# The turned residual in the place of the rounded sums, and the last round's weight sums by adding transfers

## The chip, the cores and the metric

The kernel runs on one core of a Trainium2 chip. The core has a matrix engine (PE, with weight loads shown as PEld), a vector engine (DVE), a scalar engine (ACT), GpSimd (POOL) and SyncE (SP). In this kernel SP and POOL do little but issue transfers (DMA). All engines work in the order in which their instructions stand, and wait for each other by semaphores. The metric is the device time of one execution in microseconds (us), the median of several.

## The reference

A trunk of two residual layers over 512 tokens of width 1024, in float32. Layer 0 mixes tokens by banded attention, layer 1 by a gated linear recurrence (RG-LRU). Behind each mixer stands the same MLP, and the change lies in the MLPs alone:

```python
for layer in range(2):
    h = h + mixer(rmsnorm(h, norm_mix[layer]))
    z = relu(rmsnorm(h, norm_mlp[layer]) @ w1[layer])     # 512x1024 @ 1024x4096
    h = h + (z * z) @ w2[layer]                           # 512x4096 @ 4096x1024
return rmsnorm(h, norm_final)
```

## The kernel before, in words

Each float32 product is made of three matmuls of rounded operands: every operand is split into a high part (a cast to float32r on ACT, tiles `wh`, `hnH`, `rH`, `h`, `hs`) and the rest (a subtraction on DVE, `wl`, `hnL`, `rL`, `l`, `ls`). Function `mm3`, lines 280 to 282, issues the three. So each weight block that is used costs ACT a cast (L178) and DVE a subtraction (L183), and both must be there before PE can use it.

In an MLP, `mlp(ly, norm)`, the residual is held with features in partitions (`hT`, two buffers `hx0` and `hx1`). The 4096 hidden features are 8 groups of 512. Group 0 is made plainly by four calls `up(0, j)`. The other seven (`group(p, g)`) and the whole down product use a seven-product scheme for two by two blocks: blocks of weights are called `11`, `12`, `21`, `22`, and beside them sums of blocks are multiplied. In the up products the right operand's sums are `rF[1]` to `rF[4]`, made in place of the residual (`right`) and split into `rH` and `rL` (`right_split`); they are used by the pieces `r1` to `r4` of every group. The weights' sums there are `s1` to `s4`; a tile `kept` holds `s1` and `22`, tiles `u` hold `11` and `12`.

The down product runs in four rounds p = 0 to 3, `round_(p)`. Each uses blocks `b11`, `b12`, `b22`, `b21` of `w2` (two halves of 128x1024 each, 512 KB per half) and four sums `t1` = 12 + 11, `t2` = 22 + t1, `t3` = t2 - 11, `t4` = 21 + t2. `load_down` loads a block on SP's queue; `first_sum` makes `t1` by a transfer on POOL's queue that adds one tile to another; `fetch` makes `t2` and `t3` by DVE (L173, L176) and `t4` by an adding transfer (L174). Rounds 0 to 2 alternate with the pieces of two up groups; round 3 has nothing beside it. A step of a round multiplies into PSUM banks `x`, `y` or `z`, which DVE adds to the result `d` (`read`, L747).

`fetch` is called three blocks ahead of use, and five buffers each hold the split weights `wh` and `wl`. `plan` is the list of blocks in order. Within this, a tile framework sets each engine's order by its own costs, and a tile that takes the place of another waits until all that read the other are done.

At the beginning of an MLP the residual is also turned to have tokens in partitions, as the start of the result `d` (function `turn`, called behind `up(0, 0)`): 16 DVE transposes of 128x256 (L733) into two tiles `turned`, then 32 transfers of 64 KB, 16 on SP's queue and 16 on POOL's (L740). The two tiles lie in the places of `b12` and `b22`, so those blocks can be loaded only once the 32 transfers have read them. `rH` has a place of its own of the same 16 KB per partition.

Of the kernel before, what the change touches and what calls it, by code (L numbers as in the profile page):

```python
# [10 lines left out]
F32 = mybir.dt.float32  # L11
F32R = mybir.dt.float32r
# [3 lines left out]
P = 128  # L16
# [24 lines left out]
def trunk(ctx: ExitStack, tc: tile.TileContext, xT, cols, gfin, win, wqkv, wo, rwin, rga, rgx, rwo, w1, w2, out):  # L41
# [61 lines left out]
    def two(t):  # L103
        return t.rearrange("p (k c) -> p k c", k=2)
# [4 lines left out]
    def rows(src):  # L109
        return src.rearrange("(k p) c -> p k c", p=P)  # L110

    def load_down(key, name):
        if key not in down:
            return
        both = state["raw"].tile([P, 2, 1024], F32, name=f"b{name}_{key[0]}{key[1]}", tag=f"b{name}")
        for h in range(2):
            raws[name, h] = both[:, h]
            nc.sync.dma_start(two(raws[name, h]), rows(down[key][name][h * U : (h + 1) * U]))

    def first_sum(key):  # L120
        if key in down:
            for h in range(2):
                G.dma_start(raws["12", h], raws["11", h], accum_op=ALU.add)

    def load_up(key, name):
        if key not in upper:
            return
        if name in ("s1", "22"):
            raw = state["kept"][:, int(name == "22")]
        else:  # L130
            n = state["base"] + int(name == "12")
            raw = wraw.tile([P, 1024], F32, name=f"u{name}_{key[0]}{key[1]}", tag=f"wr{n % 3}")
        raws["u" + name] = raw
        nc.sync.dma_start(four(raw), rows(upper[key]["21" if name == "s1" else name]))
        if name == "s1":
            G.dma_start(four(raw), rows(upper[key]["22"]), accum_op=ALU.add)

    def fetch():
        i = state["next"]
        state["next"] += 1  # L140
        kind, nk, key = plan[i]
        H = wsp.tile([P, 1024], F32R, name=f"wh{i}", tag="wh")
        L = wsp.tile([P, 1024], F32R, name=f"wl{i}", tag="wl")
        n, half = 1024, nk
        if kind[:5] == "plain":
            n = nk * sum(src.shape[1] for src in key)
            raw = wraw.tile([P, 1024], F32, name=f"wr{i}", tag=f"wr{state['plain'] % 3}")
            state["plain"] += 1
            rv = raw[:, :n].rearrange("p (k c) -> p k c", k=nk)
            c0 = 0  # L150
            for n_, src in enumerate(key):
                w = src.shape[1]
                queue = nc.scalar if i == 0 and n_ else nc.sync
                queue.dma_start(rv[:, :, c0 : c0 + w], rows(src))
                c0 += w
        elif kind[0] == "u":
            nk = 4
            following = (key[0], key[1] + 1)
            if kind == "us2":
                raws["us2"] = wraw.tile([P, 1024], F32, name=f"us2_{key[0]}{key[1]}", tag=f"wr{(state['base'] + 2) % 3}")  # L160
                tc.keep_in_program_order(V.tensor_add(raws["us2"], raws["u11"], raws["us1"]))
                raws["us3"] = raws["u11"]
                G.dma_start(four(raws["us3"]), rows(upper[key]["21"]), accum_op=ALU.add)
            if kind == "us4":
                raws["us4"] = raws["u12"]
                V.tensor_add(raws["us4"], raws["us4"], raws["us2"])
            raw = raws[kind]
        else:
            nk = 2
            following = (key[0], key[1] + 1)  # L170
            raw = raws[{"t1": "12", "t2": "22", "t3": "11", "t4": "21"}.get(kind, kind), half]
            if kind == "t2":
                V.tensor_add(raw, raw, raws["12", half])  # L173
                G.dma_start(raws["21", half], raw, accum_op=ALU.add)  # L174
            if kind == "t3":
                V.tensor_sub(raw, raws["22", half], raw)  # L176
        if i:
            high = S.copy(H[:, :n], raw[:, :n])  # L178
            if kind in ("us1", "us3", "t1", "t4"):
                tc.keep_in_program_order(high)  # L180
        else:
            start_.append(V.tensor_copy(H[:, :n], raw[:, :n]))
        low = V.tensor_sub(L[:, :n], raw[:, :n], f(H[:, :n]))  # L183
        if not i:
            start_.append(low)
        if kind == "plain_":
            state["base"] = state["plain"] % 3
            load_up((nk_layer[i], 0), "11")
            load_up((nk_layer[i], 0), "12")
        elif kind == "us2" and key[1]:  # L190
            load_up(following, "s1")
        elif kind == "us3":
            load_up(following, "11")
        elif kind == "us4":
            load_up(following, "12")
        elif kind == "u22" and key[1]:
            load_up(following, "22")
        elif kind == "t2" and half:
            load_down(following, "12")
        elif kind == "t3" and half:  # L200
            load_down(following, "11")
        elif kind == "t4" and half:
            first_sum(following)
            load_down(following, "22")
            load_down(following, "21")
        state["ready"].append((nk, H[:, :n].rearrange("p (k c) -> p k c", k=nk), L[:, :n].rearrange("p (k c) -> p k c", k=nk)))

# [465 lines left out]
    def mlp(ly, norm):  # L673
        with ExitStack() as mctx:
# [3 lines left out]
            xs = [(hnH[k], hnL[k]) for k in range(KT)]  # L678
            res = dp.tile([P, 4, 2, T], F32, name=f"d{ly}", tag="d")
            dt = {(t, c): res[:, t, c] for t in range(4) for c in range(2)}  # L680
            rH = zp.tile([P, 4, 4, U], F32R, name=f"rH{ly}", tag="rH")
            rL13 = zp.tile([P, 2, 4, U], F32R, name=f"rL13{ly}", tag="rL")
            low_, high = hB[0], hB[1]
            rF = {1: low_[:, :, LO], 3: low_[:, :, HI], 4: high[:, :, LO], 2: high[:, :, HI]}
# [11 lines left out]
                    V.scalar_tensor_tensor(rF[n], rF[1 if n == 2 else 2], -1.0, rF[n], ALU.mult, ALU.subtract)  # L696

            def right_split(n):
                if n == 2:
                    rL24 = per.tile([P, 2, 4, U], F32R, name=f"rL24{ly}", tag="hx0")  # L700
                    rL.update({2: rL24[:, 0], 4: rL24[:, 1]})
                H = rH[:, n - 1]
                S.copy(H, rF[n])
                V.tensor_sub(rL[n], rF[n], f(H))

            def operand(n):
                if n[0] == "r":
                    H, L = rH[:, int(n[1]) - 1], rL[int(n[1])]
                    return [(H[:, k], L[:, k]) for k in range(4)]
                ks, c = (range(4) if n[0] == "1" else range(4, KT)), (LO if n[1] == "1" else HI)  # L710
                return [(hnH[k][:, c], hnL[k][:, c]) for k in ks]
# [15 lines left out]


            def turn():
                blocks = [sr.tile([P, 2, 4, KT, 32], F32, name=f"turned{ly}{h}", tag=f"b{n}2") for h, n in enumerate((1, 2))]  # L730
                for k in range(KT):
                    for h in range(2):
                        V.transpose(  # L733
                            blocks[h].rearrange("p t j k a -> p (t j) k a")[:, :, k],
                            hT[k][:, h * U : (h + 1) * U].rearrange("p (n b) -> p n b", b=32),
                        )
                for h in range(2):
                    for i in range(4):
                        for j in range(4):
                            (G if j % 2 else nc.sync).dma_start(  # L740
                                res[32 * j : 32 * j + 32, 2 * h : 2 * h + 2, i // 2, (i % 2) * U : (i % 2 + 1) * U],
                                blocks[h][32 * i : 32 * i + 32, :, j].rearrange("p t k a -> p t (k a)"),
                            )
# [39 lines left out]
            def first():  # L783
                state["kept"] = sr.tile([P, 2, 1024], F32, name=f"kept0{ly}", tag="b21")
                load_up((ly, 0), "s1")
                load_up((ly, 0), "22")
                for j in range(4):
                    up(0, j)
                state["kept"] = per.tile([P, 2, 1024], F32, name=f"kept{ly}", tag="hx1")
                load_up((ly, 1), "s1")  # L790
                load_down((ly, 0), "11")
                load_down((ly, 0), "12")
                first_sum((ly, 0))
                here = group(0, 1)
                next(here)
                opening(0)
                next(here)
                load_down((ly, 0), "22")
                for n in range(4):
                    next(here)  # L800
                load_down((ly, 0), "21")
                load_up((ly, 1), "22")
                next(here)
                sums(0, False)
                sums(0, True)
                lengths()
# [468 lines left out]
```

## Time and profile before

| | |
|---|---|
| time, median of 3 runs | 1044.04 us (1043.4 to 1046.31) |
| the profiled execution: time / span | 1043.58 / 1041.8 us |
| mean granted PE clock | 0.994 |
| busy: PE, DVE, ACT, POOL | 1024.3, 875.2, 665.4, 91.2 us |
| transfers | 147.33 MB, mean 141 GB/s |

Times in the views count from the span's start; the profiled execution's own time lies 1.78 us above its span. A row of the timeline gives start, duration, engine, line and what the instruction writes and reads; the bracket is the idle time of the engine just before and what ended it. "SPq" and "POOLq" rows are transfers being issued, not being carried out.

### The profile page before, as it was taken

The page shows a single profiled execution, that of the slowest core. Times are in us where ns is not written, and L with a number is a line of the kernel's source. Part 1 is how long each engine was busy: PE and PEld are TensorE (multiplying, and loading weights), DVE is VectorE, ACT ScalarE, POOL GpSimd, SP SyncE. Part 2 cuts the span into 40 slices and gives each one's busy share as a digit, 9 for nine tenths or more (in the row PEclk, how much of TensorE's full clock was granted, in tenths as well). Part 3 has the DMA queues.
Part 4 walks back from the last instruction along what each step waited for, and adds up shares of the span by engine and source line. Part 5 has one row for each costly group of instructions (what it writes and reads, how often), then busy time and mean ns, then how long its engine had stood idle before and what let it go on. Part 6 is the DMA issues. An engine that isn't in the chain of part 4 may idle for free.

```text
span 1041.8 us, 15285 instructions
## 1 busy us (share of the span) xinstructions
PE 1024.3 (98%) x5762; PEld 894.6 (86%) x5762; DVE 875.2 (84%) x1230; ACT 665.4 (64%) x1020; POOL 91.2 (9%) x120
## 2 busy tenths in 40 slices
PE   9999999999989999999999999999999999999996
PEld 8888888888979999999987788888999999999985
DVE  7998778869579899799789999888589798798697
ACT  7666556647477557557556686656586566566465
POOL 1000000003101111111000000003101111111000
PEclk9999999999999999999999999999999999999998
DMA  8444354245928828818603422284928738737412
GB/s 269 118 126 137 82 158 126 62 140 135 267 66 215 230 42 208 236 41 206 199 12 100 139 61 75 60 243 122 281 52 232 203 69 215 203 62 201 122 46 96
DMA packets 122729, 147.33 MB, mean 141 GB/s; under 512 B 6304, under 2 KB 94368, under 8 KB 122656
## 3 DMA queue, kind: packets, MB, share of 16 engines
q1 hardware_dynamic: 101664, 112.09, 34.5%
q0 software_dynamic: 20416, 33.56, 18.6%
q8 instruction: 45, 0.74, 0.3%
q10 hardware_dynamic: 576, 0.72, 0.2%
q14 instruction: 28, 0.23, 0.1%
HBM read 119.07 MB, written 2.10 MB: 116 GB/s over the span
## 4 chain that ended last, share of the span: by engine, by line
PE 86%; DVE 5%; DMA 3%; ACT 3%; issue 2%; ACTq 0%; DVEq 0%; SPq 0%
PE m L282 8%; PE m L281 8%; PE m L280 8%; PE x L280 5%; PE x L281 5%; PE x L282 5%; PE y L281 4%; PE y L282 4%; PE y L280 4%; DMA u<-in_w 2%; DVE wl L183 2%; PE x L506 2%; PE wo L280 1%; PE wo L281 1%; PE ro L282 1%
## 5 line engine op out<-in xcount | busy, mean ns | idle before, releaser
L183 DVE TENSOR_TENSOR wl<-b,wh 128x1024 fp32r<-128x1024 f32 x112 | 135.8, 1220 | 37.1 <-ACT wh L178 37.0
L178 ACT CAST wh<-b 128x1024 fp32r<-128x1024 f32 x112 | 116.3, 1050 | 66.1 <-PE m L281 18.9
L282 PE MATMUL m<-rH,wl 128*128 128x256 f32 x448 | 126.2, 282 | 0.0
L281 PE MATMUL m<-rL,wh 128*128 128x256 f32 x448 | 126.2, 282 | 0.0
L280 PE MATMUL m<-rH,wh 128*128 128x256 f32 x448 | 126.1, 282 | 0.0
L178 ACT CAST wh<-wr 128x1024 fp32r<-128x1024 f32 (+1 forms) x65 | 66.8, 1030 | 47.8 <-PE wo L281 11.7
L282 PE MATMUL m<-hnH,wl 128*128 128x256 f32 x336 | 95.0, 283 | 0.0
L281 PE MATMUL m<-hnL,wh 128*128 128x256 f32 x336 | 95.0, 283 | 0.0
L280 PE MATMUL m<-hnH,wh 128*128 128x256 f32 x336 | 94.9, 282 | 0.0
L281 PEld LDWEIGHTS m<-rL,wh 128*128 128x128 f32 x448 | 85.4, 191 | 1.2
L280 PEld LDWEIGHTS m<-rH,wh 128*128 128x128 f32 x448 | 85.3, 190 | 1.1
L282 PEld LDWEIGHTS m<-rH,wl 128*128 128x128 f32 x448 | 85.3, 190 | 0.0
L183 DVE TENSOR_TENSOR wl<-wr,wh 128x1024 fp32r<-128x1024 f32 (+1 forms) x66 | 78.0, 1186 | 8.6 <-ACT wh L178 8.1
L178 ACT CAST wh<-u 128x1024 fp32r<-128x1024 f32 x56 | 58.2, 1050 | 34.5 <-PE x L282 16.9
L183 DVE TENSOR_TENSOR wl<-u,wh 128x1024 fp32r<-128x1024 f32 x56 | 67.6, 1218 | 9.8 <-ACT wh L178 9.8
L281 PEld LDWEIGHTS m<-hnL,wh 128*128 128x128 f32 x336 | 64.3, 191 | 0.8
L280 PEld LDWEIGHTS m<-hnH,wh 128*128 128x128 f32 x336 | 64.2, 191 | 0.8
L282 PEld LDWEIGHTS m<-hnH,wl 128*128 128x128 f32 x336 | 64.3, 191 | 0.0
L280 PE MATMUL x<-wh,h 128*128 128x512 f32 (+1 forms) x132 | 51.3, 388 | 3.2 <-DVE d L1049 1.8
L280 PE MATMUL y<-wh,hs 128*128 128x512 f32 x128 | 50.5, 394 | 2.7 <-ACT wh L178 2.7
L281 PE MATMUL y<-wl,hs 128*128 128x512 f32 x128 | 50.5, 394 | 1.4 <-DVE wl L183 1.4
L281 PE MATMUL x<-wl,h 128*128 128x512 f32 (+1 forms) x132 | 51.3, 389 | 0.0
(382 smaller groups left out, 2897.1 us busy)
## 6 DMA issues: line engine op xcount, KB each, us to landing
b<-in_w SPq DMA_DIRECT2D x64, 512.0 KB, 6.3
b<-b POOLq DMA_DIRECT2D x32, 512.0 KB, 7.7
kept<-in_w SPq DMA_DIRECT2D x28, 512.0 KB, 4.2
u<-in_w SPq DMA_DIRECT2D x28, 512.0 KB, 6.4
wr<-in_wqkv SPq DMA_DIRECT2D x20, 512.0 KB, 4.2
wr<-in_rwin SPq DMA_DIRECT2D x16, 512.0 KB, 3.6
kept<-in_w POOLq DMA_DIRECT2D x14, 512.0 KB, 8.1
u<-in_w POOLq DMA_DIRECT2D x14, 512.0 KB, 7.9
```

The lines of the kernel that those rows point to most:

```text
L178: high = S.copy(H[:, :n], raw[:, :n])
L183: low = V.tensor_sub(L[:, :n], raw[:, :n], f(H[:, :n]))
L280: PE.matmul(acc, WH, XH, start=start, stop=False, skip_group_check=more)
L281: PE.matmul(acc, WH, XL, start=False, stop=False, skip_group_check=more)
L282: PE.matmul(acc, WL, XH, start=False, stop=stop, skip_group_check=more)
L506: PE.transpose(b[:, c : c + P], pt[:, seg[t] + kt * P : seg[t] + (kt + 1) * P], ident)
```

## The change

The two tiles `turned` become one, in the place of `rH`. `rH` is allocated later, at the first `right_split`, and so its first cast waits until the 32 transfers have landed. `b12` and `b22` are free at the layer's beginning; the loads of `b11` and `b12` and the first sum are called before the four `up(0, j)`, the load of `b22` after `opening(0)`. In round 3 of each layer `t2` and `t3` are no longer made by DVE: once block 11 has been split, its tile is overwritten by block 22 from memory and block 12 is added to it by a transfer (that is t3 = 22 + 12), and once block 22 has been split, `t1` is added to its tile by a transfer (that is t2). In rounds 0 to 2 the sums are made as before.

```diff
             if kind == "t2":
-                V.tensor_add(raw, raw, raws["12", half])
+                if key[1] < 3:
+                    V.tensor_add(raw, raw, raws["12", half])
                 G.dma_start(raws["21", half], raw, accum_op=ALU.add)
-            if kind == "t3":
+            if kind == "t3" and key[1] < 3:
                 V.tensor_sub(raw, raws["22", half], raw)
...
-            if kind in ("us1", "us3", "t1", "t4"):
+            if kind in ("us1", "us3", "t1", "t4") or kind in ("t2", "t3") and key[1] == 3:
                 tc.keep_in_program_order(high)
...
+        elif kind in ("11", "t1", "22", "21", "t2", "t3", "t4") and key[1] == 3:
+            hs = slice(half * U, (half + 1) * U)
+            if kind == "t1":
+                nc.sync.dma_start(two(raws["11", half]), rows(down[key]["22"][hs]))
+                G.dma_start(two(raws["11", half]), rows(down[key]["12"][hs]), accum_op=ALU.add)
+            elif kind == "22":
+                G.dma_start(raws["22", half], raws["12", half], accum_op=ALU.add)
...
-            rH = zp.tile([P, 4, 4, U], F32R, name=f"rH{ly}", tag="rH")
+            turned = zp.tile([P, 2, 2, 4, KT, 32], F32, name=f"turned{ly}", tag="rH")
+            rights = []
...
             def right_split(n):
+                if n == 1:
+                    rights.append(zp.tile([P, 4, 4, U], F32R, name=f"rH{ly}", tag="rH"))
...
-                blocks = [sr.tile([P, 2, 4, KT, 32], F32, name=f"turned{ly}{h}", tag=f"b{n}2") for h, n in enumerate((1, 2))]
+                blocks = [turned[:, h] for h in range(2)]
...
                 load_up((ly, 0), "22")
+                load_down((ly, 0), "11")
+                load_down((ly, 0), "12")
+                first_sum((ly, 0))
                 for j in range(4):
                     up(0, j)
                 state["kept"] = per.tile([P, 2, 1024], F32, name=f"kept{ly}", tag="hx1")
                 load_up((ly, 1), "s1")
-                load_down((ly, 0), "11")
-                load_down((ly, 0), "12")
-                first_sum((ly, 0))
                 here = group(0, 1)
                 next(here)
                 opening(0)
-                next(here)
                 load_down((ly, 0), "22")
-                for n in range(4):
+                for n in range(5):
                     next(here)
```

The order in which the built program's instructions stand on SP at the beginning of layer 0's MLP, before. Names carry the layer and the group or round (`b12_00` is block 12 of layer 0, round 0; `u11_01` is block 11 of layer 0, the second group; `kept0` belongs to that group, `kept00` to the first).

```order
L118 DMA b11_00_2764<-in_w2 128x2x512 x2
L134 DMA u11_00_2502<-in_w1 128x4x256
L134 DMA u12_00_2504<-in_w1 128x4x256
L740 DMA d0_2550<-turned00_2588 32x2x256 x8
L740 DMA d0_2550<-turned01_2589 32x2x256 x8
L118 DMA b12_00_2767<-in_w2 128x2x512
L134 DMA kept0_2761<-in_w1 128x4x256
L118 DMA b12_00_2767<-in_w2 128x2x512
L118 DMA b22_00_2843<-in_w2 128x2x512 x2
L134 DMA kept0_2761<-in_w1 128x4x256
L134 DMA u11_01_2816<-in_w1 128x4x256
L134 DMA u12_01_2851<-in_w1 128x4x256
```

The same place on SP after the change:

```order
L118 DMA b11_00_2557<-in_w2 128x2x512 x2
L134 DMA u11_00_2502<-in_w1 128x4x256
L118 DMA b12_00_2560<-in_w2 128x2x512 x2
L134 DMA u12_00_2504<-in_w1 128x4x256
L118 DMA b22_00_2811<-in_w2 128x2x512 x2
L751 DMA d0_2550<-turned0_2551 32x2x256 x16
L134 DMA kept0_2768<-in_w1 128x4x256 x2
L134 DMA u11_01_2818<-in_w1 128x4x256
L134 DMA u12_01_2850<-in_w1 128x4x256
```

Four loads, the two halves of `b12` and of `b22`, have moved from behind the sixteen transfers of the turned residual to ahead of them. On POOL the two transfers of `first_sum` have likewise moved ahead of its sixteen.

ACT in the same stretch, before (`rH` are the casts of the four right sums, `a` the hidden features of `up(0, j)`, `m` the first copy of a bank in the second group):

```order
L703 CAST rH_2551<-h_1539 128x1024 x2
L703 CAST rH_2551<-h_1540 128x1024
L760 ACTIVATE a_0_2582<-u_2642 128x256
L760 ACTIVATE a_0_2585<-u_2642 128x256
L761 ACTIVATE a_0_2582<-a_0_2582 128x256
L761 ACTIVATE a_0_2585<-a_0_2585 128x256
L703 CAST rH_2551<-h_1540 128x1024
```

ACT after the change, where these casts now stand:

```order
L714 CAST rH_2758<-h_1539 128x1024
L771 ACTIVATE a_0_2590<-u_2729 128x256
L771 ACTIVATE a_0_2593<-u_2729 128x256
L772 ACTIVATE a_0_2590<-a_0_2590 128x256
L772 ACTIVATE a_0_2593<-a_0_2593 128x256
L714 CAST rH_2758<-h_1539 128x1024
L714 CAST rH_2758<-h_1540 128x1024 x2
L850 COPY m_2773<-m_2771 128x512
```

The four casts stood around the second call of `up`; now the first stands between the third and the fourth, and three behind the fourth. On DVE the four subtractions `rL` moved along, and the 16 transposes, which stood in groups of 2, 3, 3 and 8 between the additions that complete the residual's last columns, now all stand behind the last of these additions (3, then one `hnL`, then 13).

DVE in round 3 of layer 0, before (`wl136` belongs to the second half of block 21, `wl137` to the first half of `t2`):

```order
L183 TENSOR_TENSOR wl136_5400<-b21_03_5150,wh136_5399 128x1024
L173 TENSOR_TENSOR b22_03_5147<-b22_03_5147,b12_03_4930 128x1024
L747 SCALAR_TENSOR_TENSOR d0_2550<-y030_5317,nrq_98,d0_2550 128x512
L870 TENSOR_TENSOR ls23_0_5436<-s23_0_5278,hs203_5435 128x1024
L183 TENSOR_TENSOR wl137_5404<-b22_03_5147,wh137_5403 128x1024
L747 SCALAR_TENSOR_TENSOR d0_2550<-y031_5318,nrq_98,d0_2550 128x512
L173 TENSOR_TENSOR b22_03_5147<-b22_03_5147,b12_03_4930 128x1024
L176 TENSOR_TENSOR b11_03_5040<-b22_03_5147,b11_03_5040 128x1024
```

DVE at the same place after the change:

```order
L184 TENSOR_TENSOR wl136_5405<-b21_03_5149,wh136_5404 128x1024
L184 TENSOR_TENSOR wl137_5409<-b22_03_5146,wh137_5408 128x1024
L758 SCALAR_TENSOR_TENSOR d0_2550<-y030_5318,nrq_98,d0_2550 128x512
L880 TENSOR_TENSOR ls23_0_5440<-s23_0_5277,hs203_5439 128x1024
L758 SCALAR_TENSOR_TENSOR d0_2550<-y031_5319,nrq_98,d0_2550 128x512
L184 TENSOR_TENSOR wl138_5444<-b22_03_5146,wh138_5443 128x1024
L184 TENSOR_TENSOR wl139_5449<-b11_03_5039,wh139_5448 128x1024
```

The four sums of a last round are gone from DVE, and the subtraction of `t2`'s first half now stands directly behind that of block 21, ahead of the first of the two reads of `y`. On POOL the last round's adding transfers are six instead of two: two into `b11` (L203), two into `b22` (L205), then the two into `b21` that were there before (L175).

More of the change, by code (lines that the diff above doesn't have):

```diff
@@ L701, in right_split @@
                     rL.update({2: rL24[:, 0], 4: rL24[:, 1]})
-                H = rH[:, n - 1]
+                H = rights[0][:, n - 1]
                 S.copy(H, rF[n])
@@ L707, in operand @@
                 if n[0] == "r":
-                    H, L = rH[:, int(n[1]) - 1], rL[int(n[1])]
+                    H, L = rights[0][:, int(n[1]) - 1], rL[int(n[1])]
                     return [(H[:, k], L[:, k]) for k in range(4)]
```

## The prediction

> **What bounds the kernel now.** I read the page's head first, then PE's waits, then stretches of the span around them.
>
> ```profile
> span 1041.8 us, 15285 instructions
> PE 1024.3 (98%) x5762; PEld 894.6 (86%) x5762; DVE 875.2 (84%) x1230; ACT 665.4 (64%) x1020; POOL 91.2 (9%) x120
> ```
>
> PE is busy for 98% of the span and the change takes no matmul away, so nothing can be won but the 2% in which PE stands still, and what a granted clock below 1 costs. The view of waits for PE names those places:
>
> ```profile
> PE y L280 <- ACT wh L178: 2.7, 1, 2.7
> PE x L280 <- DVE d L747: 2.0, 2, 1.3
> PE x L280 <- DVE d L1049: 1.8, 1, 1.8
> ...
> PE y L281 <- DVE wl L183: 1.4, 1, 1.4
> ```
>
> The columns are total, times, longest. The first and the last row are one place, the first `y` product of layer 0's round 0 (297 to 300 us); the second is the last round of each layer; the third is the very end. Stretches of the span (length, busy time of PE, PEld, DVE, ACT, POOL, then PE's clock, the transfer engines' share, GB/s) show what stands around them:
>
> ```profile
> 242.00:250.00 8.00, 8.00 (x36) 6.56 (x35) 7.79 (x20) 6.04 (x9) 0.00 (x0) 1.00 0.01 2
> 264.00:288.00 24.00, 24.00 (x187) 23.28 (x187) 12.39 (x12) 11.93 (x19) 3.11 (x3) 1.00 1.09 296
> 295.00:300.00 5.00, 0.97 (x5) 0.46 (x4) 4.99 (x9) 5.00 (x9) 0.00 (x0) 0.97 0.01 2
> 300.00:302.00 2.00, 2.00 (x7) 1.71 (x8) 2.00 (x2) 1.28 (x2) 0.00 (x0) 0.50 0.00 0
> 302.00:304.00 2.00, 2.00 (x14) 2.00 (x14) 2.00 (x3) 1.81 (x2) 1.09 (x1) 0.71 0.26 56
> 1002.00:1030.00 28.00, 27.10 (x119) 21.57 (x118) 27.84 (x36) 16.65 (x27) 1.71 (x2) 1.00 0.20 38
> 1030.00:1035.00 5.00, 3.21 (x22) 3.01 (x21) 4.11 (x10) 1.65 (x6) 0.00 (x0) 0.86 0.54 210
> 1035.00:1040.00 5.00, 0.91 (x5) 0.61 (x3) 1.81 (x5) 2.09 (x6) 0.00 (x0) 0.50 0.48 187
> ```
>
> Transfers are idle from 242 to 250 and saturated for 24 us from 264. At 295 PE stops for 4 us, and right behind that the clock is at half. In the last round DVE is full (27.84 of 28). The timeline shows how the saturated transfers reach PE (start, duration, engine; the last row is issue to landing of the two `u` loads):
>
> ```profile
> 271.81 1.84 SPq L134 DMA_DIRECT2D u<-in_w  x2
> 278.32 1.05 ACT L178 CAST wh<-b 128x1024 fp32r<-128x1024 f32 x1 [1.34 <-PE m L281]
> 285.94 1.05 ACT L178 CAST wh<-u 128x1024 fp32r<-128x1024 f32 x1 [5.41 <-DMA u<-in_w]
> 296.92 1.99 ACT L178 CAST wh<-b 128x1024 fp32r<-128x1024 f32 x2
> 298.62 1.19 DVE L183 TENSOR_TENSOR wl<-b,wh 128x1024 fp32r<-128x1024 f32 x1
> 752.29 1.05 ACT L178 CAST wh<-u 128x1024 fp32r<-128x1024 f32 x1 [1.18 <-DMA u<-in_w]
> DMA to landing us min/median/max: 14.0/14.2/14.4
> ```
>
> ACT waits 5.41 us in order for block `u11` of the next group, which took 14 us to land; everything behind it on ACT is late, down to the cast of `t1` at 296.92 that PE waits for. Layer 1 runs the same program, waits there only 1.18 us (752.29), and its first `y` is in no row of waits: the stall is the late block and nothing else.
>
> **The change part by part.** *Loads at the layer's beginning.* Out of the saturated stretch go two halves of `b12`, two of `b22` and the two first sums: six transfers of 512 KB, 3.1 MB of the 24 us x 296 GB/s = 7.1 MB moved there. They come behind the loads at 228 to 241, into the empty 8 us; at 296 GB/s they take 10.6 us, so they end about when the turned residual begins to move. SP issues them behind waits it has anyway.
>
> *The rounded sums wait for the turned residual.* This is the new wait:
>
> ```profile
> 233.08 4.02 SPq L134 DMA_DIRECT2D u<-in_w  x2
> 247.46 2.73 DVE L733 STREAM_TRANSPOSE turned<-h 128x256 f32<-128x256 f32 x8
> 249.93 11.01 SPq L740 DMA_DIRECT2D d<-turned  x16
> 250.59 8.59 POOL L740 DMA_DIRECT2D d<-turned  x16 [17.30 <-ACT h L688]
> DMA to landing us min/median/max: 2.1/2.7/3.4
> 266.98 0.66 ACT L760 ACTIVATE a<-u 128x256 f32<-128x256 f32 x2 [3.45 <-PE u L282]
> L280 PE MATMUL m<-rH,wh x15: 278/283/283, 269.7 to 274.7; 128*128 128x256 f32 x15
> ```
>
> Before, the last transpose ended at 250.2. In the new order five more transposes of 0.34 us (2.73 / 8) stand behind the last addition, so they end at about 252.0. SP's sixteen issues then run to about 262.7, the last lands 2.7 later than its start, at about 264.9. The cast `rH` 1 (1.05 like the others of this size) ends at 266, `rL` 1 (1.2) at 267.2. PE reads them at 269.7: 2.4 us to spare. The other three casts stand behind the fourth `up`'s activations (266.98 + 1.3): ACT has done `rH` 3 and 2 by 270.2; DVE, which takes one sum of `a` and `rL` 3 first, has `rL` 2 at about 271.7. PE needs it one piece later than 269.7: 24 matmuls at 0.114 us (44 of them from 269.7 to 274.7) are 2.75, so 272.4, 0.7 us to spare. Cost 0, covered by those two pieces; if the cover goes, each us is a us of PE in each layer. ACT takes these 2.9 us out of its waits of 1.0 to 1.3 us for split buffers (the 1.34 above is the third of a row of them) and is back in its old place at the cast of 278.32.
>
> What is late next: `kept` of the second group lies where `rL` 4 reads, so its loads go out at about 273 instead of 264, ahead of `u11` on SP; `u11` itself waits for the subtraction of `us3`, now at about 275.4 instead of 271.8. A 512 KB load has a median of 4.2 to 6.4 us to landing:
>
> ```profile
> kept<-in_w SPq DMA_DIRECT2D x28, 512.0 KB, 4.2
> u<-in_w SPq DMA_DIRECT2D x28, 512.0 KB, 6.4
> ```
>
> That is 279.6 to 281.8. The cast can't start before its split buffer is free, when the fifth piece ends: 269.7 + 4 x 2.75 = 280.7. I take 281, 5 us earlier than 285.94. In layer 0 the subtraction for `y` ended 13.9 us behind the cast's start (298.62 + 1.19 - 285.94); 281 + 13.9 = 294.9, and PE arrives at 295. The stall of 2.7 + 1.4 = 4.1 us goes. With it goes the half clock: 2 x 0.50 and 2 x 0.29 us from 300 to 304 are 1.6. Bounds: 0 if `u11` lands no earlier, 5.7 if all goes. I take 5.7. For layer 1 I take 0, as its wait costs PE nothing now; its margins are the same two as above.
>
> *The last rounds.* Each layer loses four DVE operations and gains four adding transfers and two loads:
>
> ```profile
> 985.68 1.22 DVE L183 TENSOR_TENSOR wl<-b,wh 128x1024 fp32r<-128x1024 f32 x1 [1.65 <-ACT wh L178]
> 998.00 2.35 DVE L183 TENSOR_TENSOR wl<-b,wh 128x1024 fp32r<-128x1024 f32 x2
> 1007.27 1.22 DVE L173 TENSOR_TENSOR b<-b,b 128x1024 f32<-128x1024 f32 x1
> 1019.15 1.22 DVE L176 TENSOR_TENSOR b<-b,b 128x1024 f32<-128x1024 f32 x1
> 1009.08 0.86 POOL L174 DMA_DIRECT2D b<-b  x1 [38.13 <-DVE b L173]
> DMA to landing us min/median/max: 4.5/4.7/4.9
> b<-b POOLq DMA_DIRECT2D x32, 512.0 KB, 7.7
> 1020.29 1.40 DVE L747 SCALAR_TENSOR_TENSOR d<-x,nrq,d 128x512 f32<-128x512 f32 x2
> 1033.25 0.39 PE x L280
> ```
>
> On a full DVE one operation of this size takes 1.13 us (a pair 2.35, one alone 1.22), so four are 4.5 us per layer. PE's waits for `d` L747 follow a DVE that is behind: at 1019.15 L176 stands just ahead of the read at 1020.29. They go: 1.3 in layer 0, 0.7 in layer 1. At the end PE waits 1.8 us for L1049, which stood behind four scalings; with DVE 4.5 us ahead it waits only for that read itself, about 0.6 (0.5 us of work and a handover): 1.2 won. The last 12 pairs of half-width products then ran at half clock from 1033.25 to 1035.9, 2.7 us for 12 matmuls that take 12 x 0.114 = 1.4 at full clock. With a gap of 0.6 I take the clock as held: 1.3 won; bounds 0 and 1.3. [...]
>
> Will the sums by transfer be there? The transfer for `t2` goes out when the subtraction of block 22 is done: its first half is the second of the pair at 998.00, done by 1000.4. Alone, such a transfer lands in 4.5 to 4.9 us, in the median over the kernel 7.7. What could keep it company, the loads and sums for `t3`, goes out from the split of block 11 on (985.68 + 1.22 for its second half), 13 us earlier. So I take the near row, 4.7: 1005.1, and the cast is done when DVE comes to it at 1007.3. Cost 0; if it takes 7.7, DVE, in order, waits 2 us and half its gain is lost. The sums into `b21` can only come earlier than before.
>
> The sum: 4.1 + 1.6 (layer 0's beginning) + 1.3 (layer 0's last round) + 0.7 + 1.2 + 1.3 (layer 1's) = 10.2 us. The profiled execution took 1043.58: 1033.4. The median of the runs, 1044.04, lies 0.46 above that execution, so a median may come out as much higher.
>
> **The rivals.** *The sums land late* (10 in 100). For it: the median of 7.7 and a DVE that is never free. Against it: the two at the end took 4.5 to 4.9. DVE would wait for `t2` in order, the reads stay late, and the last rounds win nothing: 1043.58 - 5.7 = 1037.9. POOL issued L174 in 0.86 us while DVE was full (27.84 of 28). [...]
>
> *`u11` is late again* (10 in 100): `kept` now goes out later and just ahead of it. For it: loads among others took 14 us here. Against it: half of that traffic is gone. From a landing at 281 on each us is a us of PE, up to the old 4.1; the clock then stays as it was too: 1043.58 - 4.5 = 1039.1.
>
> *Slower: POOL stands still behind the first sum* (6 in 100). Its sixteen transfers of the turned residual now stand behind the two sums that wait for `b12`. If `b12` landed late, all `rH` would be. Up to a start on POOL at about 254.8 (252.4 and the spare 2.4) nothing happens; from there each us costs a us of PE in each layer, and 1.6 of clock once the gap is 4 us. At a start of 260 that is 5.2 + 1.6, twice, 13.6 against 10.2 won: 1047.0. It decides from about 258.4. Against it: SP issues `b12` behind the `u` load at 233, and before, all that stood in the queue had landed by 242.
>
> *No effect* (4 in 100): the stalls turn into others of the same size, 1043.6.
>
> **How the numbers follow.** My forecast holds 70 in 100, 15 of them for a last half clock that stays (1034.7), with a range of its own from 1030.5 (other small gaps of PE behind DVE go too) to 1035.5 (a us of new wait in each opening). The range from 1030.0 to 1039.5 takes in the first two rivals and leaves out the last two. About 0.3% (3 us) is what a measurement here can tell from no change. Faster: 70, 10 and 10 less 3 for mishaps together, 0.87. Same: 0.05. Slower: 0.08.
>
> **What would show it.** Right: no wait of PE for `y` near 295 and a clock of 1.00 through 300 to 304; the transfers' share near 1 from 242 to 250 and below it around 280; ACT's wait for `u` under 1 us; `rH` at 265 without a wait of PE for `m`; no L173 or L176 in the last rounds and no wait of PE for L747 there; a last gap of about 0.6 us. Wrong: PE waiting for `rL` or `rH` near 270 or 740, DVE waiting for a transfer `b` near 1005, or `u` landing behind 281.

## The result, and the profile after

| kernel | median, us | runs, us | ratio to the kernel before (95% interval) |
|---|---|---|---|
| before | 1044.47 | 1043.4 to 1046.31 | |
| changed | 1036.03 | 1034.71 to 1036.72 | 0.9916 (0.9898 to 0.9934) |
| changed, a second time | 1035.39 | 1034.41 to 1037.94 | 0.9924 (0.9909 to 0.9938) |

The change makes the kernel about 0.8% faster. The forecast was 1033.4 with a range from 1030.0 to 1039.5, so the time lies inside it, 2.6 us above the point. The profiled execution took 1035.93 us, 7.65 below the one before. The head of its page:

```profile
span 1034.2 us, 15261 instructions
PE 1021.6 (99%) x5762; PEld 892.5 (86%) x5762; DVE 866.8 (84%) x1222; ACT 665.7 (64%) x1020; POOL 99.4 (10%) x128
```

PE does the same 5762 matmuls. DVE is busy for 8.4 us less, and POOL issues eight transfers more. PE's waits, in the same view as before (total, times, longest); in the changed kernel `mm3` is L288 to L290, L714 and L715 make `rH` and `rL`, and L850 copies the bank `m`:

```profile
PE m L289 <- DVE rL L715: 0.9, 1, 0.9
PE x L288 <- DVE d L1059: 0.6, 1, 0.6
PE m L288 <- ACT rH L714: 0.6, 1, 0.6
...
PE m L288 <- ACT m L850: 0.4, 2, 0.2
```

The waits for `y` (2.7 and 1.4 us) and the two for `d` in the last rounds (2.0) are gone, and the one at the very end has gone from 1.8 to 0.6. In their place stand three rows on `m`, which were not there before. The first two are in layer 1, where PE waits for the rounded sums `rH` and `rL` themselves. The third has one wait in each layer: the copy of `m` stands on ACT behind the late casts of `rH`. The same stretches as before (length, busy time of PE, PEld, DVE, ACT, POOL, PE's clock, transfer engines' share, GB/s). The last three are taken 8 us earlier; the program runs 4.2 us earlier when the last round begins and 7.7 at the very end, so they do not hold quite the same work:

```profile
242.00:250.00 8.00, 8.00 (x36) 6.53 (x35) 6.90 (x17) 5.32 (x8) 1.58 (x2) 1.00 1.08 288
264.00:288.00 24.00, 23.76 (x183) 22.80 (x182) 16.42 (x16) 19.46 (x33) 1.31 (x1) 1.00 0.65 171
295.00:300.00 5.00, 5.00 (x40) 4.78 (x39) 5.00 (x6) 4.10 (x5) 1.14 (x1) 1.00 0.10 21
300.00:302.00 2.00, 2.00 (x10) 1.66 (x9) 1.97 (x3) 1.81 (x4) 0.15 (x1) 1.00 0.85 240
...
994.00:1022.00 28.00, 28.00 (x124) 22.90 (x124) 26.80 (x34) 19.90 (x30) 3.50 (x4) 1.00 0.42 85
1022.00:1027.00 5.00, 4.42 (x28) 3.83 (x27) 4.27 (x9) 2.42 (x8) 0.00 (x0) 1.00 0.40 155
1027.00:1032.00 5.00, 1.03 (x9) 0.82 (x7) 2.05 (x7) 2.15 (x6) 0.00 (x0) 1.00 0.47 179
```

The early loads fill the once empty 242 to 250 (share 0.01 before, 1.08 now), and 264 to 288 is no longer saturated (0.65 for 1.09). PE has no hole from 295 on, the clock stays at 1.00, and in the last round DVE has 1.2 us to spare where it had 0.2.

What PE wins and loses is best counted by its matmuls: both traces have 5762, in the same order but for 52 places, so the start of the nth in one can be set against the start of the nth in the other. Between the two profiled executions this gives 6.0 us won from 293 to 314 (the stall for `y` and the half clock behind it), 1.3 in layer 0's last round, 0.3 at layer 1's first `y` near 766, and 3.5 in layer 1's last round, but 0.8 us newly lost around 272 and 2.7 around 740 (times of the trace of before). That makes 7.6, which is the whole difference of the spans. Where a single gap of PE is given below, it is counted from the start of one matmul to the start of the next, less the usual 0.12 or 0.23 us (for 256 or 512 columns).

### The profile page after: what moved, and what is told of

The parts are those of the page before. It is cut to its first block, busy times and chain, and to the rows that moved or that the text cites. A ratio compares the mean times of both kernels' runs of the same rounds, so it can differ in the third digit from the quotient of the medians.

```text
span 1034.2 us, 15261 instructions
## 1 busy us (share of the span) xinstructions
PE 1021.6 (99%) x5762; PEld 892.5 (86%) x5762; DVE 866.8 (84%) x1222; ACT 665.7 (64%) x1020; POOL 99.4 (10%) x128
## 4 chain that ended last, share of the span: by engine, by line
PE 82%; DVE 7%; DMA 5%; ACT 2%; SPq 2%; issue 1%; DVEq 0%; ACTq 0%
PE m L289 9%; PE m L288 9%; PE m L290 9%; PE x L288 6%; PE x L289 6%; PE x L290 6%; PE y L288 4%; PE y L289 4%; PE y L290 4%; DVE wl L184 2%; PE x L514 1%; PE v L288 1%; DMA wr<-in_w 1%; PE v L290 1%; PE yb L290 1%; PE v L289 1%
## 5 line engine op out<-in xcount | busy, mean ns | idle before, releaser
L288 PE MATMUL m<-rH,wh 128*128 128x256 f32 x448 | 126.1, 281 | 1.0 <-ACT rH L714 0.6
L290 PE MATMUL m<-rH,wl 128*128 128x256 f32 x448 | 125.9, 281 | 0.0
L290 PE MATMUL m<-hnH,wl 128*128 128x256 f32 x336 | 95.0, 283 | 0.0
L288 PE MATMUL m<-hnH,wh 128*128 128x256 f32 x336 | 94.9, 282 | 0.0
L288 PEld LDWEIGHTS m<-rH,wh 128*128 128x128 f32 x448 | 84.8, 189 | 2.6 <-ACT m L850 0.8
L290 PEld LDWEIGHTS m<-rH,wl 128*128 128x128 f32 x448 | 84.9, 189 | 0.0
L288 PEld LDWEIGHTS m<-hnH,wh 128*128 128x128 f32 x336 | 64.2, 191 | 0.8
L290 PEld LDWEIGHTS m<-hnH,wl 128*128 128x128 f32 x336 | 64.3, 191 | 0.0
L288 PE MATMUL x<-wh,h 128*128 128x512 f32 (+1 forms) x132 | 50.9, 386 | 0.6 <-DVE d L1059 0.6
L290 PE MATMUL x<-wh,l 128*128 128x512 f32 (+1 forms) x132 | 50.9, 385 | 0.0
L288 PE MATMUL y<-wh,hs 128*128 128x512 f32 x128 | 50.2, 392 | 0.0
```

The source lines that it names most:

```text
L288: PE.matmul(acc, WH, XH, start=start, stop=False, skip_group_check=more)
L290: PE.matmul(acc, WL, XH, start=False, stop=stop, skip_group_check=more)
```

## The experiments

The first four ran together on one chip, the last four on another; each is compared with the kernel before on its own chip (1043.15 and 1042.91 us).

| kernel | median, us | ratio (95% interval) |
|---|---|---|
| openings alone | 1039.77 | 0.9968 (0.9955 to 0.9980) |
| last rounds alone | 1038.53 | 0.9957 (0.9945 to 0.9970) |
| a pool of its own | 1032.96 | 0.9902 (0.9887 to 0.9917) |
| without the `u` sum | 1032.61 | 0.9898 (0.9885 to 0.9912) |
| changed, again | 1035.39 | 0.9924 (0.9909 to 0.9938) |
| a pool of its own, again | 1032.19 | 0.9892 (0.9877 to 0.9906) |
| loads late again | 1036.79 | 0.9937 (0.9922 to 0.9951) |
| without the last sums | 1035.65 | 0.9928 (0.9912 to 0.9943) |

Set against the kernel before matmul by matmul, the traces agree closely. Each run with the whole new opening wins 6.0 us at layer 0's stall (with the loads late again 3.8), and each run with the new last rounds wins 1.3 and 3.5 us in them. What differs most from run to run is the new wait for the rounded sums.

**The openings alone.** `fetch` and its loads are those of before; `turned`, `rH` and `first()` those of the changed kernel.

```diff
             if kind == "t2":
-                if key[1] < 3:
-                    V.tensor_add(raw, raw, raws["12", half])
+                V.tensor_add(raw, raw, raws["12", half])
...
-            if kind == "t3" and key[1] < 3:
+            if kind == "t3":
...
-        elif kind in ("11", "t1", "22", "21", "t2", "t3", "t4") and key[1] == 3:
...
```

> The change at the layers' beginnings alone; the last rounds' sums are made by DVE as before. Reading the trace of the changed kernel, the last rounds won 1.6 us in layer 0 and 3.4 us in layer 1, so this kernel should stand 5.0 us above the changed kernel, 1041.0, and show the openings of the changed kernel: no wait of PE for y in layer 0, and PE waiting for rH and rL near 272 (some 0.7 us) and near 735 (some 2.5 us). By the terms of the forecast (opening 5.7 us against the kernel before, new wait 0) it would be 1038.8. If the two parts hinder each other, the sum of this gain and that of the last rounds alone differs from 8.4 us by more than 1 us.

Measured: 0.32% faster, 3.4 us, where 3.5 were expected (1041.0 against 1044.5). Its PE waits:

```profile
PE x L280 <- DVE d L750: 2.1, 2, 1.3
PE x L280 <- DVE d L1051: 1.8, 1, 1.8
...
PE m L281 <- DVE rL L707: 0.9, 1, 0.9
```

No wait for `y`, the old waits of the last rounds, the new wait for `rL`: as expected (0.8 us lost in layer 0, and 1.9 in layer 1, where 2.5 were expected). One thing was not: the last gap is as long as before, and yet the clock does not fall behind it (the last section comes back to it).

**The last rounds alone.** The reverse: `fetch` as changed, the openings as before.

```diff
-            turned = zp.tile([P, 2, 2, 4, KT, 32], F32, name=f"turned{ly}", tag="rH")
-            rights = []
+            rH = zp.tile([P, 4, 4, U], F32R, name=f"rH{ly}", tag="rH")
...
-                blocks = [turned[:, h] for h in range(2)]
+                blocks = [sr.tile([P, 2, 4, KT, 32], F32, name=f"turned{ly}{h}", tag=f"b{n}2") for h, n in enumerate((1, 2))]
```

> The last rounds alone; the openings are as before. Theory: the gain of the last rounds comes only from DVE being 4.5 us ahead there, and needs nothing of the openings: 5.0 us below the kernel before, 1039.5; the stall of PE for y near 297 and the half clock behind it stay, the gap at the very end falls from 1.9 to about 0.7 us and the last products run at full clock. By the forecast's own terms 4.5 us, 1040.0. Rival: the adding transfers cost something that the saturated transfers of the openings hide: 1042 or more.

Measured: 0.43% faster, 4.5 us, where 5.0 were expected and the forecast's own terms gave 4.5. In its trace PE waits for `y` by 3.0 and 1.2 us in layer 0, and by 0.6 for the last read. The two parts add up: 3.4 + 4.5 = 7.9 us, and the whole change wins 7.9 on the second chip (1042.91 x 0.0076). By the intervals, which leave about 1.5 us either way, no hindrance of one part by the other can be seen.

**A pool of its own.** Same tiles, same addresses; only the pool from which the place is taken is another.

```diff
-            sr, zp, dp = (... for n in ("sr", "z", "d"))
+            sr, rp, zp, dp = (... for n in ("sr", "r", "z", "d"))
-            turned = zp.tile([P, 2, 2, 4, KT, 32], F32, name=f"turned{ly}", tag="rH")
+            turned = rp.tile([P, 2, 2, 4, KT, 32], F32, name=f"turned{ly}", tag="rH")
...
-                    rights.append(zp.tile([P, 4, 4, U], F32R, name=f"rH{ly}", tag="rH"))
+                    rights.append(rp.tile([P, 4, 4, U], F32R, name=f"rH{ly}", tag="rH"))
```

> The changed kernel, with the turned residual and the rounded sums in a pool of their own, at the same addresses. Theory: the pool that they lie in now spans the operands of the mixer's last product, so the 16 transposes are put behind all of the mixer, and that made the transfers of the turned residual start 5 us late in layer 1 and 1.4 in layer 0. With a pool of its own the transposes go back between the last additions, rH 1 is cast at about 728 (not 733) and at about 266 (not 267.3) relative to the same program, and PE's waits for rH and rL (some 0.9 and 2.5 us) go: 1032.6. Rival one: the transfers' end is set by the adding transfer of u behind them on POOL's queue, wherever they start; then only a part goes, 1034 to 1035. Rival two: rH is late because of where its casts stand on ACT: 1036.0, no change.

Beside the changed kernel on one chip:

> The place in a pool of its own once more, beside the changed kernel on one chip. In the first run its trace had no wait of PE for rH or rL left, and a new wait of 0.4 us for hnL in layer 1. Theory: the new wait of the changed kernel costs 0.9 and 2.5 us, and this kernel wins it less 0.5: 2.9 us below the changed kernel, ratio to the kernel before about 0.9888. Rival: that wait hides other stalls behind it, and the two are within 0.5 us.

Measured: 1032.19 against 1035.39, 3.2 us, and no row of `rH` or `rL` among PE's waits in either of its traces. The first has a small new wait for `hnL` in layer 1 (0.4 us), the second has not. Layer 1's timeline (start, duration, engine) shows why, first of the changed kernel, then of this one:

```profile
710.43 0.75 DVE L1225 SCALAR_TENSOR_TENSOR t<-ro,cst,t 128x512 f32<-128x512 f32 x1
711.09 1.09 DVE L744 STREAM_TRANSPOSE turned<-t 128x256 f32<-128x256 f32 x3
...
712.73 4.36 DVE L744 STREAM_TRANSPOSE turned<-t 128x256 f32<-128x256 f32 x13
716.83 12.95 SPq L751 DMA_DIRECT2D d<-turned  x16
726.09 1.36 POOL L163 DMA_DIRECT2D u<-in_w  x1
733.25 1.05 ACT L714 CAST rH<-t 128x1024 fp32r<-128x1024 f32 x1 [4.72 <-DMA d<-turned]
```

```profile
700.88 1.09 DVE L744 STREAM_TRANSPOSE turned<-t 128x256 f32<-128x256 f32 x3
...
710.18 0.74 DVE L1225 SCALAR_TENSOR_TENSOR t<-ro,cst,t 128x512 f32<-128x512 f32 x1
710.96 0.77 DVE L744 STREAM_TRANSPOSE turned<-t 128x256 f32<-128x256 f32 x2
711.47 10.93 SPq L751 DMA_DIRECT2D d<-turned  x16
726.12 1.05 ACT L714 CAST rH<-t 128x1024 fp32r<-128x1024 f32 x1 [3.63 <-DMA d<-turned]
```

In the changed kernel all sixteen transposes stand behind the last addition (L1225) and end 5.9 us after it. With a pool of its own only two do, SP begins to issue 5.4 us earlier, and `rH` is cast 7.1 us earlier. (Some 2 us of the 7.1 seem to be of this trace alone: SP's sixteen issues took 12.95 us in it, and 10.8 in that of the openings alone, from 718.6 to 729.4.) That nothing but the grouping was changed shows the grouping to be the cause. Why it matters is read from the program and not shown by a trace: pool `z` spans addresses at which the mixer keeps the operands of its last product until that product is done, and the framework lets nothing into such a pool before; the pool of one place is free earlier.

**Without the `u` sum.** The transfer that POOL issues directly behind the sixteen turned ones (726.09 above) is left out for the first group of each layer.

```diff
                 raws["us3"] = raws["u11"]
-                G.dma_start(four(raws["us3"]), rows(upper[key]["21"]), accum_op=ALU.add)
+                if key[1]:
+                    G.dma_start(four(raws["us3"]), rows(upper[key]["21"]), accum_op=ALU.add)
```

> The changed kernel without the adding transfer of 512 KB that makes us3 of the first group in each layer (that sum is left out, so group 0's second-round operand u is not the right one; all other work is done). It is issued on POOL directly behind the sixteen turned transfers, and in the trace the last turned transfers of SP took 5.1 us to land where others took 2.8, while that queue filled the transfer engines from 264 to 265. Theory (crowding): without it the last turned transfer lands 2.3 us earlier, rH 1 is cast at about 265 and 731, the waits of PE for rH 1 and rL 1 in layer 1 (1.9 us) go, those behind the fourth up's activations (0.7 us per layer) stay: 1034.1. Rival (only the late start of the transfers counts): the time stays at 1036.0 and the last turned transfer takes 5 us all the same.

Measured: 1032.61, with no wait for `rH` or `rL` left: crowding is shown, and it costs more than expected. In layer 0 the changed kernel's rows (the timeline; the packets, MB and share of the engines from 264 to 265 by queue; the landings of the turned transfers) are

```profile
251.38 10.94 SPq L751 DMA_DIRECT2D d<-turned  x16
260.64 1.36 POOL L163 DMA_DIRECT2D u<-in_w  x1
267.26 1.05 ACT L714 CAST rH<-h 128x1024 fp32r<-128x1024 f32 x1 [3.88 <-DMA u<-in_w]
```

```profile
q0 software_dynamic: 177, 0.18, 118.3%
q1 hardware_dynamic: 2, 0.00, 0.9%
```

```profile
DMA to landing us min/median/max: 2.1/2.8/5.1
```

and without the sum

```profile
264.14 1.05 ACT L715 CAST rH<-h 128x1024 fp32r<-128x1024 f32 x1 [0.85 <-DMA d<-turned]
```

```profile
DMA to landing us min/median/max: 2.0/2.7/3.6
```

POOL's queue (q0) took the engines whole (118.3%, a share above 100% since the packets' times overlap) while SP's last turned transfer (q1, 0.9%) stood. Issued at 261.73, it landed 5.1 us later and so ended the wait of `rH` 1; the bracket of that row names the sum into `u`, which happened to land then too. (The cast reads nothing of `u`; in the trace of the openings alone its row, at 267.21, names `DMA d<-turned`.) Without the sum SP's last one landed in 2.0 us, and `rH` 1 is cast 3.1 us earlier in layer 0, and in layer 1 at 728.82 for 733.25. In layer 1 the longest landing is 5.0 us even without the sum (5.2 with it), but it is that of an earlier transfer: SP's last one took 2.6 instead of 4.8. I had expected 0.7 us per layer to stay, for the three casts that stand behind the fourth `up`'s activations. They went too: those activations stand behind `rH` 1 in ACT's order, so they had only been late with it.

**Loads late again.** `turned` stays in the new place, but the loads of `b12` and `b22` are called behind `turn()` and held there on SP, with `first_sum` behind them.

```diff
-            nc.sync.dma_start(two(raws[name, h]), rows(down[key][name][h * U : (h + 1) * U]))
+            load = nc.sync.dma_start(two(raws[name, h]), rows(down[key][name][h * U : (h + 1) * U]))
+            if key[1] == 0 and name in ("12", "22"):
+                tc.keep_in_program_order(load)
...
-                load_down((ly, 0), "12")
-                first_sum((ly, 0))
                 for j in range(4):
                     up(0, j)
+                    if j == 0:
+                        load_down((ly, 0), "12")
+                        load_down((ly, 0), "22")
+                        first_sum((ly, 0))
...
-                load_down((ly, 0), "22")
```

> The changed kernel (turned residual in the place of the rounded sums), but the loads of b12 and b22 are held behind the sixteen turned transfers on SP, where the kernel before had them, and first_sum comes behind them. Theory A (the early loads free u11): the transfers are saturated again from 262 on, u11 of the second group lands late, ACT waits over 3 us for it in layer 0, and PE waits for y near 297 by 2 us or more: 2 to 6 us above the changed kernel. Theory B (u11 is freed by the order on SP, since kept and u11 now stand behind the read of rL 4 and go out only at 274, when these loads are done): no wait for y, within 1 us of the changed kernel. Both: the turned transfers may land later still, with loads beside their last ones, which would show as a longer wait for rH.

Its stretches, ACT's cast of `u11` and PE's waits:

```profile
264.00:288.00 24.00, 23.98 (x185) 23.16 (x184) 16.55 (x16) 17.00 (x27) 3.08 (x3) 1.00 1.07 285
295.00:300.00 5.00, 3.33 (x22) 2.67 (x21) 5.00 (x8) 4.76 (x6) 0.00 (x0) 1.00 0.00 2
```

```profile
284.41 1.05 ACT L181 CAST wh<-u 128x1024 fp32r<-128x1024 f32 x1 [3.06 <-DMA u<-in_w]
```

```profile
PE y L291 <- DVE wl L186: 2.7, 2, 1.4
```

The saturation is back (1.07), `u11` is late by 3 us, and PE waits for `y` again, 2.1 us in layer 0 and 2.0 in layer 1 from start to start. So the early loads do free `u11` (theory A). Part of the old stall does not return: `u11` now goes out later but lands in 7.6 us, not 14. In time the kernel stands 1.4 us above the changed one, less than the 2 to 6 us of theory A, with intervals that overlap. In its trace the new wait for the rounded sums is shorter, by 0.4 us in layer 0 and 1.0 in layer 1 against the first trace of the changed kernel. Its traced execution was the slowest of its six (1039.23), so the trace carries this point and not the median.

**The changed kernel again.** 

> The changed kernel once more, so that it shares a chip and the runs of the kernel before with the three kernels beside it. Its ratio to the kernel before was 0.9916 (0.9898 to 0.9934); expected within that, and PE waiting for rH and rL by some 0.7 us in layer 0 and 2.5 us in layer 1.

Measured as expected, but for layer 0: in this trace the wait near 272 is not there at all, and only that in layer 1 is (2.4 us). In layer 0 the margin is used up to the last tenths: over the four traces with this opening (twice the changed kernel, the openings alone, without the last sums) PE loses 0.8, 0, 0.8 and 0.4 us there.

**Without the last sums.** The loads and adding transfers of the last round are taken out of the changed kernel, so that two of its seven products take other operands.

```diff
-            hs = slice(half * U, (half + 1) * U)
-            if kind == "t1":
-                nc.sync.dma_start(two(raws["11", half]), rows(down[key]["22"][hs]))
-                G.dma_start(two(raws["11", half]), rows(down[key]["12"][hs]), accum_op=ALU.add)
-            elif kind == "22":
-                G.dma_start(raws["22", half], raws["12", half], accum_op=ALU.add)
+            pass
```

> The changed kernel without the last rounds' loads and adding transfers for t2 and t3 (their sums are left out altogether, by DVE and by transfer, so two of the seven products take other operands; all other work is done). Theory: those transfers are hidden, as forecast at cost 0: the same time as the changed kernel within 0.5 us. Rival: they cost what ACT waited for them in the trace (1.1 us in two places) or more: 1 to 2 us below the changed kernel.

Measured: 1035.65 against 1035.39. The medians alone would leave room for a us or two, but the traces do not: the last rounds win 1.3 and 3.5 us over the kernel before in both. The transfers cost PE nothing.

## Why the prediction was right, and where it was off

*Loads at the layer's beginning, 5.7 us: right.* 6.0 us were won. `kept` went out at 274.36 (forecast 273), `u11` at 276.63 (275.4), and its cast started at 281.95 (281); it waited 0.67 us for a split buffer, not for the block. The late loads show the mechanism.

*The rounded sums wait for the turned residual, cost 0: wrong.* This is the term that was mis-sized. Taking it away won 3.2 us on one chip (the pool of its own against the changed kernel), and the trace shows 0.8 us in layer 0 and 2.7 in layer 1. PE waiting for `rH` or `rL` near 270 or 740 was one of the prediction's own signs of being wrong, and in layer 1 it came. Two steps of the term failed.

- "The last lands 2.7 later than its start, at about 264.9." Up to that step the working held: transposes done at 251.6 (forecast 252.0), SP's last issue over at 262.3 (262.7). But the landing took up to 5.1 us, and `rH` 1 was cast from 267.3 instead of 265. I had counted the sixteen transfers on each queue, and not what POOL issues next, the 512 KB sum into `u`. It is in the trace of before too, issued at 260.17; but there SP's last turned transfer went out 0.2 us behind it, at 260.35, and landed in 2.2 us, while in the changed kernel it went out 1.1 us behind it (261.73 and 260.64). This used up layer 0's 2.4 us: PE found `rH` 1 done at 269.5, and lost its 0.8 us near 272.4, at the copy of `m` that ACT makes behind the three late casts.
- For layer 1, "its margins are the same two as above". I had looked at the moved transposes in layer 0, where they end 1.4 us later. In layer 1 most of them had been done before the last addition:

```profile
700.01 1.09 DVE L733 STREAM_TRANSPOSE turned<-t 128x256 f32<-128x256 f32 x3
...
715.76 0.75 DVE L1215 SCALAR_TENSOR_TENSOR t<-ro,cst,t 128x512 f32<-128x512 f32 x1 [0.24 <-PE ro L282]
716.55 0.77 DVE L733 STREAM_TRANSPOSE turned<-t 128x256 f32<-128x256 f32 x2
```

That is the kernel before: the transposes end 0.8 us behind the last addition, in the changed kernel 5.9. So the move cost 5.1 us there. From the end of the transposes to the moment at which PE is ready for `rH` (about 733.6, `rH` 1 is done at 734.3) are 16.5 us in layer 1 and 17.9 in layer 0 (251.6 to 269.5). The crowding then did the rest. Either of the two, taken away, removes the wait: without the sum the transposes are as late as in the changed kernel, and with a pool of its own SP's last turned transfer still takes 4.7 us in layer 0. Each had used up the margin only together with the other.

The forecast's own range took in "a us of new wait in each opening", which was too little in layer 1.

*The last rounds, 1.3 + 0.7 + 1.2 + 1.3 us: right in sum, one term for a poor reason.* The waits for L747 went (gaps of 1.4 us in layer 0 and 1.2 in layer 1), and the last gap went from 1.95 to 0.74. The clock's share was won in this pair of traces too, 0.8 us where 1.3 were taken. That the shorter gap won it is not shown, and in part it is luck: with the openings alone the long gap stays, the clock does not fall behind it, and the same 0.8 us are won.

*Sums by transfer, cost 0: right.* The two sums for `t2` in layer 1 were issued at 996.42 and 998.74:

```profile
996.42 0.89 POOL L205 DMA_DIRECT2D b<-b  x1 [8.04 <-DVE wl L184]
...
1001.07 1.06 ACT L179 CAST wh<-b 128x1024 fp32r<-128x1024 f32 x1 [0.55 <-DMA b<-b]
```

```profile
DMA to landing us min/median/max: 4.6/4.8/5.0
```

All four landed in 4.6 to 5.0 us (4.7 was taken), and ACT waited half a us.

Of the rivals, none came. *The sums land late* would have shown DVE waiting near 1005, but they landed in time with DVE busy for 26.80 of 28 us. *`u11` late again* did not happen, since the cast waited for its buffer. *POOL stands still behind the first sum*: it issued both sums by 244.04 and its first turned transfer at 252.03, ahead of the 254.8 up to which nothing was to happen. *No effect* did not come either, since the interval of the ratio ends at 0.9934. The measured terms are 6.0 + 1.3 + 3.5, and 0.3 at layer 1's first `y`, which the sum did not have: 11.1 for the forecast's 10.2. Less 3.5 of new wait, where 0 was taken, this is the 7.6 by which the traces differ. Without the wait the forecast would have been 0.9 us too high; with it, it was 2.5 too low for the traced execution, and the range was wide enough for that.

## What to carry to other kernels

When a tile takes another's place, the cost is not the copy but the last of everything that must be over first: follow that chain to the last packet, with whatever the other queues issue next, and do it anew for every layer, because the scheduler's order differs from one to the next. Look at which pool the place comes from: here the same tiles at the same addresses came free earlier when their place had a pool of its own, and in the large pool they seem to have waited for neighbours with which they share no byte. That version is the fastest that was run with nothing left out, 0.9892 (0.9877 to 0.9906).

## What the runs showed of the hardware

**In two traces the granted clock changed after whole multiples of 3.4133 us.** In the trace of before it was full for 293.546 us (86 times 3.4133), half for 3.413 and full for 730.452 (214 times); in the changed kernel's it was full for 1027.412 (301 times). From the span's start the changes lie elsewhere in each: at 299.74, 303.15 and 1033.61 before, and at 1032.39 in the changed kernel, which is 214.6 times 3.4133 behind 299.74. With the openings alone the clock fell at about 1035.45 (its mean is 0.91 from 1033 to 1036); stretches of 3.413 us are counted back from there. The same gap of 1.95 us fell into one such stretch before, and across the border of two with the openings alone; the stretches around it (columns as above), first before, then the openings alone:

```profile
1030.19:1033.61 3.42, 1.63 (x14) 1.43 (x13) 3.01 (x5) 0.71 (x3) 0.00 (x0) 1.00 0.74 284
```

```profile
1025.22:1028.63 3.41, 2.42 (x17) 2.06 (x15) 3.41 (x8) 0.00 (x0) 0.00 (x0) 1.00 0.41 156
1028.63:1032.04 3.41, 1.69 (x12) 1.49 (x12) 2.47 (x7) 2.05 (x7) 0.00 (x0) 1.00 0.40 151
```

Behind the first, with PE busy for 1.63 of 3.42 us, the clock was halved; behind 2.42 and 1.69 of 3.41 it was not. The half clock cost 0.8 us at the end of the program: the last matmuls stand 0.21 us apart before and 0.12 in the changed kernel. With the openings alone a gap of the same length cost nothing. That the place of the gap decided this is my estimate from these two traces, as no run moved the gap alone. Whether PE's busy time decides it is not shown either, as 1.63 and 1.69 lie close together.

**In one stretch POOL's queue had the transfer engines nearly to itself.** From 264 to 265 of the changed kernel's trace POOL's queue moved 177 packets and SP's two, though SP's last turned transfer (64 KB) had been issued at 261.73; from 265 to 267 SP's queue moved 78 packets, 0.06 MB. No run here shows why, nor whether SP's packets were ready to go in that time.
